# An RWKV/gMLP trunk: projections as 512-column products per channel tile, and six row copies a batch moved from ScalarE to DMA

## The chip, the cores and the metric

One core of one Trainium2 chip runs the kernel. The metric is the device time of one execution in microseconds (us). TensorE (PE) multiplies, VectorE (DVE) and ScalarE (ACT) do the elementwise work, GpSimd (POOL) a little of it, SyncE (SP) issues most DMAs. Products land in PSUM, whose banks hold 512 float32 numbers in each of 128 partitions; everything else lies in SBUF.

## The reference

The input is 256 tokens of width 2048 in float32. Two residual layers follow each other, then a last RMS norm.

```python
def rwkv7_bidir_mixer(h, w_in, mu_prev, mu_next, ...):      # layer 0
    z = h @ w_in                       # 2048 -> r, k, v (4096 each), 4 low-rank inputs of 96, gate (4096)
    zs, gate = z[..., :SHIFT_COLS], z[..., SHIFT_COLS:]
    zs = zs + mu_prev * (shift_prev(zs) - zs) + mu_next * (shift_next(zs) - zs)
    ...
    for d, rev in ((0, False), (1, True)):                  # one scan per direction, 64 heads of 64
        # S_t = S_{t-1} diag(w_t) + (S_{t-1} a_t) b_t^T + v_t k_t^T ;  y_t = S_t r_t
        y = y + wkv_scan(rh, heads(decay), kd_h, vh, -kk, kk * a_h, rev)
        bonus = bonus + jnp.sum(rh * kd_h * r_k, axis=-1, keepdims=True) * vh
    ...                                                     # group norm of y, plus bonus
    return (out * jax.nn.silu(gate)) @ w_out                # 4096 -> 2048

def chunked_sgu_mixer(h, w_in, ln_g, ln_b, w_s, b_s, w_out):  # layer 1
    u, v, gate = jnp.split(h @ w_in, 3, axis=-1)            # 2048 -> 3 x 4096
    ...                                                     # spatial mix of v in chunks of 128 tokens
    return (u * s * jax.nn.silu(gate)) @ w_out
```

## The kernel before

**Precision by three products.** Every float32 operand of a large product is split into a hi and a lo part of type float32r. `mm3` (L163) adds up hi·hi, lo·hi and hi·lo in one PSUM bank. The activations of layer 0 are split into `zT`, two tiles `zh` and `zl` of 16 k-tiles by 256 tokens.

**Weights.** `want` queues up a piece of a weight matrix, `prefetch` keeps three pieces ready, `fetch` hands out the next. `convert` (L133) makes one: a DMA on SP's queue into one of two raw buffers (L145; L143 for the low-rank ones), a cast on ScalarE to the hi part (L150), a subtraction on VectorE for the lo part (L151). A raw buffer is free for the next DMA when L151 has read it. A piece holds 1024 numbers per partition, 512 KB. `want_cols` (L173) cuts a column range of a weight matrix into such pieces; for a width of 256 it is four k-tiles of 256 columns, in runs of 1 KB.

**Rounds.** The 4096 channels are worked on in 16 batches of 256 (two channel tiles of 128, four heads). Round p of the loop at L909 interleaves generators, each of which yields its due time within a round of nominally 78: the projections (`mains`) of k and r of batch p and of v and gate of batch p-1; `rates`, `factors` and `early_grams` of batch p; `before` (grams of the second direction, then `inverses`), `values` and `transposed_factors` of batch p-1; `after` (the scan over four chunks of 64 tokens, `chain`, then `finish`) of batch p-2. The due times set the order in which instructions are written; a scheduler then orders each engine's queue by its own model of the times. Each engine, and SP's DMA queue, works through its queue in order.

**A projection.** `mains` takes one PSUM bank for a segment of a batch: 256 tokens of the first channel tile, then 256 of the second. `project` (L179) runs the 16 k-tiles, and for each the two channel tiles, three products of 256 columns each:

```python
mm3(acc, (hi[:, j, cs], lo[:, j, cs]), (zT[0][:, k], zT[1][:, k]), k == 0 and i % 2 == 0, k == KT - 1)
```

Two banks of the tag "acc" alternate. Then `shifted` (L390 to L399) makes the token shift for r, k and v straight from PSUM: for each channel tile one ScalarE activation and two VectorE steps. The gate takes one activation (L450) and one VectorE step (L451) over both tiles.

**The wide product.** In layer 1, u and gate use `project_wide` (L194). There the activations lie as hi and lo side by side, so that hi weights meet 512 columns at once (L204) and lo weights only the 256 hi columns (L206). Its two halves are then summed by a ScalarE copy (L1065) and a VectorE add (L1066).

**The inverses.** `inverses` (L611) copies 32-row blocks of the gram matrix `Gs` to `Dt` (L623) and `NQ` (L624), solves for triangular inverses on VectorE (L627 to L643), finishes off the off-diagonal block by products into `qp` (L651, L657), and puts together `TTs` from `qp` (L660) and from the transposed `TD` (L661, L662). All these copies move 32 partitions by 512 numbers and run on ScalarE. `TTs` is one buffer, read by `chain` at L722 (`uu`). `values` (L684) then has SP's queue overwrite half of `Gs` from `AR`, which must wait for the copies out of `Gs`, and fill `RC`.

Of the kernel before, what the change touches and what calls it, by code (L numbers as in the profile page):

```python
# [22 lines left out]
def trunk(tc, x, norm_g, final_norm_g, w_in, mu_prev, mu_next, w0, w_up, a0, a_up, k_k, k_a, r_k,  # L23
# [149 lines left out]
    def want_cols(w, c_off, b, name):  # L173
        a = min(KT, 1 << int(math.log2(RAW // b)))
        wv = w.rearrange("(k p) c -> p k c", p=P)
        for k0 in range(0, KT, a):
            want(wv[:, k0:k0 + a, c_off:c_off + b], a, b, f"{name}{k0}")
# [32 lines left out]

    def acc_pair(name):
        return sm(name, "acc").rearrange("p (i t) -> p i t", i=2)
# [69 lines left out]
    zT = (zp.tile([P, KT, T], F32R, tag="zh", name="zh"), zp.tile([P, KT, T], F32R, tag="zl", name="zl"))  # L282
# [73 lines left out]
    for todo in plan:  # L356
        for s, b in todo:
            if s == "u":
                want([w_[0, :, :, b * 2 * P:(b + 1) * 2 * P].rearrange("d k c -> k d c") for w_ in (w_up, a_up)],
                     4, 2 * P, f"wu{b}")  # L360
            else:
                want_cols(w_in, segment[s] + b * 2 * P, 2 * P, f"w{s}{b}_")
# [27 lines left out]
    def shifted(acc, dst, b, m):  # L390

        for cl in range(2):
            a = acc[:, cl]
            j = m * NCT + 2 * b + cl
            S.activation(dst[:, cl], a, AF.Identity, scale=c0[:, j:j + 1])
            V.scalar_tensor_tensor(dst[:, cl, 1:], a[:, :T - 1], col["mp"][:, j:j + 1], dst[:, cl, 1:],
                                   ALU.mult, ALU.add)
            V.scalar_tensor_tensor(dst[:, cl, :T - 1], a[:, 1:], col["mn"][:, j:j + 1], dst[:, cl, :T - 1],
                                   ALU.mult, ALU.add)  # L399
# [36 lines left out]
    def mains(todo, st):  # L436
        slot = dict(k=0, r=4, g=12, v=8) if "k" in dict(todo) else dict(v=0, g=4)
        last = -4
        for s, b in todo:
            if s == "u":  # L440
                st[b]["wu"] = fetch()
                continue
            last = max(last + 4, slot[s])
            yield last * MT
            acc = acc_pair(f"acc{s}{b}")
            for i, _ in enumerate(project(2 * P, [acc[:, 0], acc[:, 1]], zT)):
                yield last * MT + i * dt
            if s == "g":
                SG = fr.tile([P, 2, T], F32, tag="SG", name=f"SG{b}", bufs=2)
                S.activation(SG, acc, AF.Tanh, scale=0.5)  # L450
                V.scalar_tensor_tensor(SG, SG, 1.0, acc, ALU.add, ALU.mult)  # L451
                st[b]["SG"] = SG
            elif s == "v":
                Vt = fr.tile([P, 2, T], F32, tag="Vt", name=f"Vt{b}", bufs=2)
                shifted(acc, Vt, b, 2)
                st[b]["Vt"] = Vt
            else:
                t = fr.tile([P, 2, T], F32, tag=f"{s}t", name=f"{s}t{b}")
                shifted(acc, t, b, dict(r=0, k=1)[s])
                st[b][dict(r="Rt", k="Kt")[s]] = t  # L460
# [150 lines left out]
    def inverses(b, f):  # L611
# [8 lines left out]
        for h in range(2):  # L620
# [3 lines left out]
            S.copy(NQ[h * 64:h * 64 + 32], Gs[0:32, h, :, 32:64])  # L624
# [30 lines left out]
        for u in range(16):  # L655
            for h in range(2):
                PE.matmul(qp[R0[h], u], NQ[R1[h], u], TD[R1[h], u], start=True, stop=True)  # L657
        yield TQ[1] + 2
        for h in range(2):
            S.copy(TTs[R0[h], h, :, 32:64], qp[R0[h]])  # L660
            S.copy(TTs[R0[h], h, :, 0:32], TD[R0[h]])  # L661
            S.copy(TTs[R1[h], h, :, 32:64], TD[R1[h]])  # L662
# [206 lines left out]
    def early_out():  # L869

        yield 4
        oA = [zp.tile([P, HE, T], F32R, tag=t, name=f"{t}_o0") for t in ("zh", "zl")]
# [196 lines left out]
    pA = [zp.tile([P, HE, T], F32R, tag=t, name=f"{t}_o1") for t in ("zh", "zl")]  # L1069
# [101 lines left out]
```

## Time and profile before

| | |
|---|---|
| median of 3 runs | 2230.92 us (2229.87 to 2234.58) |
| the profiled execution | 2229.16 us |
| its span, first to last instruction | 2227.4 us |
| mean granted TensorE clock | 0.995 |
| TensorE / VectorE / ScalarE busy | 98% / 72% / 60% of the span |
| layer 0 with its projections | about 31 to 1290 us of the span |
| output of layer 0, then layer 1 | 1290 us to the end |

How to read the lines of a profile: L12 is line 12 of the kernel; `out<-in` names what is written and what is read. A line of a group gives the shapes, the count behind x, busy time in us, the mean duration of one in ns, then the idle time of that engine just before, and what ended it. A line of a stretch gives the busy time of each engine in it, with the number of instructions, the granted clock, the busy share of the DMA engines and GB/s. A line of a wait gives total us, number of times and the longest. A line of the timeline gives start and duration in us. A line of a DMA issue gives count, size, and median us to landing. TensorE's products overlap, so the duration of one isn't its price.

### The profile page before, as it was taken

The page shows a single profiled execution, that of the slowest core. Times are in us where ns is not written, and L with a number is a line of the kernel's source. Part 1 is how long each engine was busy: PE and PEld are TensorE (multiplying, and loading weights), DVE is VectorE, ACT ScalarE, POOL GpSimd, SP SyncE. Part 2 cuts the span into 40 slices and gives each one's busy share as a digit, 9 for nine tenths or more (in the row PEclk, how much of TensorE's full clock was granted, in tenths as well). Part 3 has the DMA queues.
Part 4 walks back from the last instruction along what each step waited for, and adds up shares of the span by engine and source line. Part 5 has one row for each costly group of instructions (what it writes and reads, how often), then busy time and mean ns, then how long its engine had stood idle before and what let it go on. Part 6 is the DMA issues. An engine that isn't in the chain of part 4 may idle for free.

```text
span 2227.4 us, 48630 instructions
## 1 busy us (share of the span) xinstructions
PE 2179.0 (98%) x19984; PEld 1944.7 (87%) x19984; DVE 1608.1 (72%) x3121; ACT 1345.2 (60%) x2128; POOL 171.8 (8%) x230
## 2 busy tenths in 40 slices
PE   7999999999999999999999999999999999999998
PEld 7889999999999999999999877778888888888886
DVE  5797788787977977887888764465546777777444
ACT  6556777777767676776767664464444444444443
POOL 2210110011001101100010000000000000000000
PEclk9999999999999999999999999999999999999999
DMA  5555444454445544444545555586766666665664
GB/s 167 140 145 142 109 126 134 125 137 112 130 127 143 139 126 131 129 125 136 137 124 138 167 174 177 173 263 189 221 204 190 198 189 195 195 193 192 195 198 154
DMA packets 352687, 356.01 MB, mean 160 GB/s; under 512 B 78160, under 2 KB 300112, under 8 KB 352336
## 3 DMA queue, kind: packets, MB, share of 16 engines
q1 hardware_dynamic: 332208, 331.66, 51.6%
q10 hardware_dynamic: 20256, 21.24, 3.2%
q8 instruction: 157, 2.57, 0.5%
q14 instruction: 66, 0.54, 0.1%
HBM read 329.78 MB, written 6.29 MB: 151 GB/s over the span
## 4 chain that ended last, share of the span: by engine, by line
PE 69%; ACT 10%; DMA 9%; DVE 8%; issue 3%; ACTq 0%; SPq 0%; POOL 0%; POOLq 0%; DVEq 0%
PE uacc L204 5%; PE gacc L204 5%; DMA raw_o<-in_rwkv_w_out_dram 3%; PE oacc L166 3%; PE oacc L167 3%; PE oacc L165 3%; PE gp L584 3%; PE gacc L206 3%; PE uacc L206 3%; PE vacc L167 3%; PE vacc L165 3%; PE vacc L166 3%; ACT Dt L623 2%; PE accv L165 2%; PE accg L167 2%
## 5 line engine op out<-in xcount | busy, mean ns | idle before, releaser
L204 PE MATMUL uacc<-z,whi_u 128*128 128x512 f32 x512 | 179.0, 394 | 0.0
L204 PE MATMUL gacc<-z,whi_g 128*128 128x512 f32 x512 | 177.3, 393 | 0.0
L167 PE MATMUL accg<-zh,wlo_wg 128*128 128x256 f32 x512 | 149.6, 292 | 2.5 <-DVE wlo_wg L151 2.4
L165 PE MATMUL accv<-zh,whi_wv 128*128 128x256 f32 x512 | 149.2, 291 | 1.1 <-ACT whi_wv L150 1.1
L167 PE MATMUL accr<-zh,wlo_wr 128*128 128x256 f32 x512 | 148.7, 290 | 0.6 <-DVE wlo_wr L151 0.5
L165 PE MATMUL acck<-zh,whi_wk 128*128 128x256 f32 x512 | 148.1, 289 | 1.1 <-ACT whi_wk L150 1.1
L165 PE MATMUL accr<-zh,whi_wr 128*128 128x256 f32 x512 | 149.0, 291 | 0.0
L165 PE MATMUL accg<-zh,whi_wg 128*128 128x256 f32 x512 | 148.4, 290 | 0.0
L166 PE MATMUL accr<-zl,whi_wr 128*128 128x256 f32 x512 | 148.1, 289 | 0.0
L167 PE MATMUL accv<-zh,wlo_wv 128*128 128x256 f32 x512 | 147.5, 288 | 0.1
L167 PE MATMUL acck<-zh,wlo_wk 128*128 128x256 f32 x512 | 146.2, 286 | 1.0 <-DVE wlo_wk L151 1.0
L166 PE MATMUL accv<-zl,whi_wv 128*128 128x256 f32 x512 | 147.2, 287 | 0.0
L166 PE MATMUL accg<-zl,whi_wg 128*128 128x256 f32 x512 | 147.0, 287 | 0.0
L166 PE MATMUL acck<-zl,whi_wk 128*128 128x256 f32 x512 | 147.0, 287 | 0.0
L206 PE MATMUL uacc<-z,wlo_u 128*128 128x256 f32 x512 | 142.4, 284 | 0.0
L206 PE MATMUL gacc<-z,wlo_g 128*128 128x256 f32 x512 | 140.2, 279 | 0.0
L151 DVE TENSOR_TENSOR wlo_v<-raw_v,whi_v 128x1024 fp32r<-128x1024 f32 x64 | 78.4, 1225 | 80.4 <-ACT whi_v L150 80.4
L151 DVE TENSOR_TENSOR wlo_o<-raw_o,whi_o 128x1024 fp32r<-128x1024 f32 x64 | 78.2, 1224 | 77.5 <-ACT whi_o L150 77.2
L639 DVE TENSOR_TENSOR X<-X,TD 128x126 f32<-128x126 f32 (+22 forms) x496 | 126.5, 255 | 9.4
L637 DVE TENSOR_TENSOR TD<-La,X 128x126 f32<-128x126 f32 (+22 forms) x496 | 125.6, 253 | 10.6
L151 DVE TENSOR_TENSOR wlo_p<-raw_p,whi_p 128x1024 fp32r<-128x1024 f32 x60 | 73.9, 1232 | 75.7 <-ACT whi_p L150 75.7
L150 ACT CAST whi_p<-raw_p 128x1024 fp32r<-128x1024 f32 x60 | 63.1, 1051 | 91.5 <-PE oacc L167 87.3
(331 smaller groups left out, 6842.3 us busy)
## 6 DMA issues: line engine op xcount, KB each, us to landing
raw_wk<-in_rwkv_w_in_dram SPq DMA_DIRECT2D x64, 512.0 KB, 3.7
raw_wr<-in_rwkv_w_in_dram SPq DMA_DIRECT2D x64, 512.0 KB, 3.7
raw_wv<-in_rwkv_w_in_dram SPq DMA_DIRECT2D x64, 512.0 KB, 3.7
raw_wg<-in_rwkv_w_in_dram SPq DMA_DIRECT2D x64, 512.0 KB, 3.7
raw_o<-in_rwkv_w_out_dram SPq DMA_DIRECT2D x64, 512.0 KB, 4.0
raw_v<-in_gmlp_w_in_dram SPq DMA_DIRECT2D x64, 512.0 KB, 3.7
raw_u<-in_gmlp_w_in_dram SPq DMA_DIRECT2D x64, 512.0 KB, 3.5
raw_g<-in_gmlp_w_in_dram SPq DMA_DIRECT2D x64, 512.0 KB, 3.6
```

What stands on the lines that cost most here:

```text
L150: latest[0] = S.copy(hi, raw)
L151: latest[1] = V.tensor_tensor(lo, raw, hi.bitcast(F32), ALU.subtract)
L165: PE.matmul(acc, a[0], b[0], start=first, stop=False, skip_group_check=True)
L166: PE.matmul(acc, a[0], b[1], start=False, stop=False, skip_group_check=True)
L167: PE.matmul(acc, a[1], b[0], start=False, stop=last, skip_group_check=True)
L204: PE.matmul(acc.rearrange("p h t -> p (h t)"), hi[:, j, cs], zc[:, k].rearrange("p h t -> p (h t)"), start=k == 0, stop=False, skip_group_ ...
L206: PE.matmul(acc[:, 0], lo[:, j, cs], zc[:, k, 0], start=False, stop=k == KT - 1, skip_group_check=True)
L584: PE.matmul(gp[h][:, c].rearrange("p q t -> p (q t)"), BK[H[h], d, cl, c].rearrange("p q t -> p (q t)"), AR[H[h], d, cl, c].rearrange("p q ...
L623: S.copy(Dt[r0:r0 + 32].rearrange("p t u -> p u t"), Gs[q * 32:q * 32 + 32, h, :, q * 32:q * 32 + 32])
L637: V.tensor_tensor(tv, La[:, j, 0:j].unsqueeze(2).to_broadcast([P, j, n]), X[:, j:j + 1, m:].to_broadcast([P, j, n]), ALU.mult)
L639: V.tensor_tensor(X[:, 0:j, m:], X[:, 0:j, m:], tv, ALU.add)
```

## The change

**Projections.** The weights of r, k, v and gate are wanted 128 columns at a time, eight k-tiles a piece, in runs of 512 bytes. `zT` becomes two views of one tile `zi` in which hi and lo lie side by side. Each channel tile takes a PSUM bank of its own and `project_wide`; a ScalarE copy and a VectorE add sum the halves into `pa` in SBUF, one buffer, from which the shift or the gate's steps work for that channel tile.

**Copies.** In `inverses`, the two copies to `NQ` and the four copies from `TD` to `TTs` become DMAs issued on SP's queue. The copies from `Gs` to `Dt` and from `qp` stay.

Later tiles that took over the space of `zh` and `zl` now take the two halves of one tile; nothing else changes there.

```diff
     def want_cols(w, c_off, b, name):
-        a = min(KT, 1 << int(math.log2(RAW // b)))
+        a = min(KT, RAW // b if b == P else 1 << int(math.log2(RAW // b)))
...
-    zT = (zp.tile([P, KT, T], F32R, tag="zh", name="zh"), zp.tile([P, KT, T], F32R, tag="zl", name="zl"))
+    zi = zp.tile([P, KT, 2, T], F32R, tag="z", name="z0")
+    zT = [zi[:, :, i] for i in range(2)]
...
-                want_cols(w_in, segment[s] + b * 2 * P, 2 * P, f"w{s}{b}_")
+                for cl in range(2):
+                    want_cols(w_in, segment[s] + (2 * b + cl) * P, P, f"w{s}{b}_{cl}")
...
-    def shifted(acc, dst, b, m):
-
-        for cl in range(2):
-            a = acc[:, cl]
-            j = m * NCT + 2 * b + cl
-            S.activation(dst[:, cl], a, AF.Identity, scale=c0[:, j:j + 1])
-            V.scalar_tensor_tensor(dst[:, cl, 1:], a[:, :T - 1], col["mp"][:, j:j + 1], dst[:, cl, 1:],
-                                   ALU.mult, ALU.add)
-            V.scalar_tensor_tensor(dst[:, cl, :T - 1], a[:, 1:], col["mn"][:, j:j + 1], dst[:, cl, :T - 1],
-                                   ALU.mult, ALU.add)
+    def shifted(a, dst, j):
+
+        S.activation(dst, a, AF.Identity, scale=c0[:, j:j + 1])
+        V.scalar_tensor_tensor(dst[:, 1:], a[:, :T - 1], col["mp"][:, j:j + 1], dst[:, 1:], ALU.mult, ALU.add)
+        V.scalar_tensor_tensor(dst[:, :T - 1], a[:, 1:], col["mn"][:, j:j + 1], dst[:, :T - 1], ALU.mult, ALU.add)
...
-            acc = acc_pair(f"acc{s}{b}")
-            for i, _ in enumerate(project(2 * P, [acc[:, 0], acc[:, 1]], zT)):
-                yield last * MT + i * dt
-            if s == "g":
-                SG = fr.tile([P, 2, T], F32, tag="SG", name=f"SG{b}", bufs=2)
-                S.activation(SG, acc, AF.Tanh, scale=0.5)
-                V.scalar_tensor_tensor(SG, SG, 1.0, acc, ALU.add, ALU.mult)
-                st[b]["SG"] = SG
...
+            tag, n = dict(k=("kt", 1), r=("rt", 1), v=("Vt", 2), g=("SG", 2))[s]
+            dst = fr.tile([P, 2, T], F32, tag=tag, name=f"{tag}{b}", bufs=n)
+            for cl in range(2):
+                acc = sm(f"acc{s}{b}_{cl}", "acc").rearrange("p (h t) -> p h t", h=2)
+                for i, _ in enumerate(project_wide(P, [acc], zi)):
+                    yield last * MT + (cl * KT + i) * dt / 2
+
+                a = fr.tile([P, T], F32, tag="pa", name=f"pa{s}{b}_{cl}")
+                S.copy(a, acc[:, 1])
+                V.tensor_tensor(a, acc[:, 0], a, ALU.add)
+                if s == "g":
+                    S.activation(dst[:, cl], a, AF.Tanh, scale=0.5)
+                    V.scalar_tensor_tensor(dst[:, cl], dst[:, cl], 1.0, a, ALU.add, ALU.mult)
+                else:
+                    shifted(a, dst[:, cl], dict(r=0, k=1, v=2)[s] * NCT + 2 * b + cl)
+            st[b][dict(r="Rt", k="Kt", v="Vt", g="SG")[s]] = dst
...
-            S.copy(NQ[h * 64:h * 64 + 32], Gs[0:32, h, :, 32:64])
+            nc.sync.dma_start(NQ[h * 64:h * 64 + 32], Gs[0:32, h, :, 32:64])
...
                 PE.matmul(qp[R0[h], u], NQ[R1[h], u], TD[R1[h], u], start=True, stop=True)
+        for h in range(2):
+            nc.sync.dma_start(TTs[R0[h], h, :, 0:32], TD[R0[h]])
+            nc.sync.dma_start(TTs[R1[h], h, :, 32:64], TD[R1[h]])
         yield TQ[1] + 2
         for h in range(2):
             S.copy(TTs[R0[h], h, :, 32:64], qp[R0[h]])
-            S.copy(TTs[R0[h], h, :, 0:32], TD[R0[h]])
-            S.copy(TTs[R1[h], h, :, 32:64], TD[R1[h]])
```

More of the change, by code (lines that the diff above doesn't have):

```diff
@@ L209, in project_wide @@
                 yield
-    def acc_pair(name):
-        return sm(name, "acc").rearrange("p (i t) -> p i t", i=2)
     n3 = 3 * NCT
@@ L444, in mains @@
             yield last * MT
-            acc = acc_pair(f"acc{s}{b}")
-            for i, _ in enumerate(project(2 * P, [acc[:, 0], acc[:, 1]], zT)):
-                yield last * MT + i * dt
-            if s == "g":
-                SG = fr.tile([P, 2, T], F32, tag="SG", name=f"SG{b}", bufs=2)
-                S.activation(SG, acc, AF.Tanh, scale=0.5)
-                V.scalar_tensor_tensor(SG, SG, 1.0, acc, ALU.add, ALU.mult)
-                st[b]["SG"] = SG
[L453 to L460, printed above, removed]
+            tag, n = dict(k=("kt", 1), r=("rt", 1), v=("Vt", 2), g=("SG", 2))[s]
[13 more added lines that the diff above has]
+            st[b][dict(r="Rt", k="Kt", v="Vt", g="SG")[s]] = dst
         if ("g", NB - 1) in todo:
@@ L871, in early_out @@
         yield 4
-        oA = [zp.tile([P, HE, T], F32R, tag=t, name=f"{t}_o0") for t in ("zh", "zl")]
+        oA = zp.tile([P, 2, HE, T], F32R, tag="z", name="z_o0")
+        oA = [oA[:, i] for i in range(2)]
         oC = sc.tile([P, 2, 16, 2 * C], F32R, tag="Gs", name="oCh", bufs=2)
@@ L1067, in gated @@
         V.tensor_tensor(dst, dst, rb2, ALU.mult)
-    pA = [zp.tile([P, HE, T], F32R, tag=t, name=f"{t}_o1") for t in ("zh", "zl")]
+    pA = zp.tile([P, 2, HE, T], F32R, tag="z", name="z_o1")
+    pA = [pA[:, i] for i in range(2)]
     pB = None
```

## The prediction

> **What bounds the kernel now.** I read the page first (busy shares, the chain that ended last), then the sums by stage, TensorE's waits in the steady part of the RWKV layer, and its timeline there and in the gMLP layer, which already has the wide product.
>
> ```profile
> span 2227.4 us, 48630 instructions
> PE 2179.0 (98%) x19984; PEld 1944.7 (87%) x19984; DVE 1608.1 (72%) x3121; ACT 1345.2 (60%) x2128; POOL 171.8 (8%) x230
> PE 69%; ACT 10%; DMA 9%; DVE 8%; issue 3%; ACTq 0%; SPq 0%; POOL 0%; POOLq 0%; DVEq 0%
> ```
>
> TensorE carries 69% of the chain. A busy TensorE alone says little, since products overlap; so the stages:
>
> ```profile
> core 0: us, PE busy (x) PEld busy (x) DVE busy (x) ACT busy (x) POOL busy (x), PEclk, DMA share, GB/s
> 58.00:290.00 232.00, 219.88 (x2330) 208.03 (x2330) 190.29 (x389) 151.57 (x248) 34.28 (x37) 0.97 0.49 134
> 600.00:1221.00 621.00, 615.91 (x7639) 574.47 (x7638) 508.87 (x1195) 442.15 (x765) 58.23 (x79) 1.00 0.50 132
> ...
> PE yp L731 <- ACT SUV L724: 2.1, 2, 1.1
> PE uu L722 <- ACT Xs L718: 1.9, 4, 0.6
> PE xp L713 <- ACT SUV L680: 0.6, 2, 0.3
> ```
>
> 600 to 1221 us holds eight rounds of one batch each, 77.6 us a round. TensorE idles 5.1 us in eight rounds, 4.6 of them in three waits on ScalarE, none on a weight. VectorE is busy 63.6 us a round (82%), ScalarE 55.3. So here a round is as long as TensorE's work in it. From 58 to 290 (rounds 1 to 3) TensorE idles 12.1 us and its clock was 0.97: there other engines still matter.
>
> **The projections.** One unit (one k-tile, one channel tile) is now three 256-column products; it becomes one of 512 and one of 256. Both exist in the trace, uninterrupted:
>
> ```profile
> 642.39 0.28 PE L165 MATMUL accr<-zh,whi_wr 128*128 128x256 f32 x1
> 642.51 0.28 PE L166 MATMUL accr<-zl,whi_wr 128*128 128x256 f32 x1
> 642.63 0.28 PE L167 MATMUL accr<-zh,wlo_wr 128*128 128x256 f32 x1
> ...
> 644.19 0.28 PE L165 MATMUL accr<-zh,whi_wr 128*128 128x256 f32 x1
> ```
>
> ```profile
> 1753.33 0.39 PE L204 MATMUL gacc<-z,whi_g 128*128 128x512 f32 x1
> 1753.56 0.28 PE L206 MATMUL gacc<-z,wlo_g 128*128 128x256 f32 x1
> ...
> 1755.07 0.39 PE L204 MATMUL gacc<-z,whi_g 128*128 128x512 f32 x1
> ```
>
> From 642.39 to 644.19 stand five old units: 360 ns each, 120 a product. From 1753.33 to 1755.07 stand five new ones: 348 ns each (231 and 117). The saving is 12 to 13 ns a unit; I take 12.5. Durations (0.28, 0.39) are not the price, the distance between starts is.
>
> ```profile
> L165 PE MATMUL acck<-zh,whi_wk 128*128 128x256 f32 x512 | 148.1, 289 | 1.1 <-ACT whi_wk L150 1.1
> L1065 ACT COPY Gt<-uacc 128x256 f32<-128x256 f32 x32 | 12.0, 374 | 16.8 <-PE uacc L206 16.8
> L1066 DVE TENSOR_TENSOR U<-uacc,Gt 128x256 f32<-128x256 f32 x32 | 13.5, 421 | 2.1 <-ACT Gt L1065 0.7
> L661 ACT COPY TTs<-TD 32x512 f32<-32x512 f32 x32 | 19.7, 615 | 17.4 <-DVE TD L642 8.0 <-PE uu L722 7.8 <-DVE nm L760 1.4
> L624 ACT COPY NQ<-Gs 32x512 f32<-32x512 f32 x32 | 19.8, 618 | 3.6 <-DVE Gs L589 3.0
> L450 ACT ACTIVATE SG<-accg 128x512 f32<-128x512 f32 x16 | 9.7, 607 | 0.1
> L451 DVE SCALAR_TENSOR_TENSOR SG<-SG,accg 128x512 f32<-128x512 f32 x16 | 10.9, 682 | 9.0 <-ACT SG L450 9.0
> L395 ACT ACTIVATE kt<-acck,c 128x256 f32<-128x256 f32 x32 | 15.3, 477 | 5.2 <-PE acck L167 3.6 <-DVE kt L398 1.3
> L492 ACT ACTIVATE SQ<-kt,pc 128x256 f32<-128x256 f32 x32 | 16.2, 506 | 2.4 <-DVE kt L398 2.4
> L568 DVE SCALAR_TENSOR_TENSOR BQ<-rt,pc,TH 128x256 f32<-128x256 f32 x32 | 14.1, 469 | 0.0
> ```
>
> 512 products of each kind and segment, four segments: 2048 units, 128 a round. 2048 x 12.5 ns = **25.6 us off TensorE**, 1.6 a round. At 98 to 99% busy that is on the path.
>
> **What it adds.** The two halves of a bank must be summed: per channel tile one ScalarE copy from PSUM (nearest row L1065, 0.374 us) and one VectorE add (L1066, 0.421); eight channel tiles a round.
> - VectorE: 8 x 0.421 = 3.4 us; the gate's 512-wide step (0.682) becomes two of 256 (L568, 0.469 each): +0.26. The shift steps stay. Together +3.6: 67.2 us a round, against 76.0 us left to TensorE, 88%.
> - ScalarE: +8 x 0.374 = 3.0; the gate's activation 0.607 becomes 2 x 0.506 (L492): +0.4; six of the shift's activations read SBUF (0.506) instead of PSUM (0.477): +0.2. Off go six copies of 0.617 (two as L624, four as L661): -3.7. Net about zero.
> - The bank: a unit row of 16 k-tiles lasts 16 x 0.348 = 5.6 us alone and 9.5 us with the other work of the round, and two banks alternate. Copy and add hold a bank 0.8 us plus two queue waits (L450 shows 9.0 us over 16 behind it). Zero. The one `pa` buffer makes the next copy wait for the shift of the last tile: copy, add, activation, two steps, 2.2 us without waits, under 9.5. If queue waits push that over 9.5 plus a bank's 5.6, TensorE stops; I leave that in the VectorE rival.
>
> What hides VectorE's 3.6 us is its idle time, 14.0 us a round (621 less 508.87, by eight), which falls to 8.8. Bounds of the cost: 0 (all hidden) to 16 x 3.6 = 58 us (none). TensorE idles 0.64 us a round today, none of it named for VectorE; if that grows as VectorE's idle shrinks, 0.64 x 14.0/8.8 = 1.0, it is +0.4 a round. Rounds 1 to 3 have less cover. I take **+6 us** in all.
>
> **Weight loads.** Each load keeps 512 KB but runs of 512 bytes (128 columns), twice as many.
>
> ```profile
> raw_wk<-in_rwkv_w_in_dram SPq DMA_DIRECT2D x64, 512.0 KB, 3.7
> RC<-AR SPq DMA_DIRECT2D x32, 256.0 KB, 5.2
> Gs<-AR SPq DMA_DIRECT2D x32, 256.0 KB, 3.7
> L684 SPq DMA_DIRECT2D Gs<-AR x32: 590/596/665, 108.5 to 1256.3; - x32
> ```
>
> The nearest rows are those two, 1024 runs of 256 bytes in 3.7 to 5.2 us, against 512 runs of 1 KB in 3.7. So a load lands 0 to 1.5 us later; I take 0.3, near the lower end, since half of the DMA time is free (share 0.50). In steady rounds it is hidden (no TensorE wait on a weight above); where two raw buffers pace the start, about a dozen loads, it is exposed: bounds 0 to 18 us, taken **+2**.
>
> **The six row copies.** The four TTs copies and two NQ copies become DMAs on SP, each 64 KB in runs of 128 bytes. Issue: 6 x 0.6 us (L684) a round, against seventeen weight issues; room enough. Landing: bounds 3.7 to 5.2 us by the rows above, against 0.617.
>
> ```profile
> 924.36 0.62 ACT L661 COPY TTs<-TD 32x512 f32<-32x512 f32 x1 [2.04 <-DVE TD L642]
> ...
> 952.50 0.69 PE L722 MATMUL uu<-Xs,TTs 128*64 128x64 f32 x16
> ...
> SPq L684 <- ACT NQ L624: 46.4, 20, 5.7
> SPq L684 <- DVE Gs L589: 19.6, 9, 5.8
> ```
>
> TTs could start at 924 and is read at 952: 28 us cover 5.2. NQ is read half a round later; but Gs<-AR overwrites what NQ copies, so SP now holds that DMA until ScalarE has done NQ (46.4 us in 20 waits). Afterwards it waits for four Dt copies and a landing instead; ScalarE ends 1.2 us earlier, the landing may take it back: zero, bounds -1 to +2 a round, off TensorE's path. What is new is order: SP waits in line for TD and the last uu before it issues the weight loads behind. Cost now: zero; see the SP rival.
> [...]
>
> **Sum**, against the profiled execution (2229.16 us, span 2227.4): 2229.2 - 25.6 + 6 + 2 = 2211.6. The median of the runs is 1.8 above it: **2213 us**, 0.8% faster.
>
> **Rivals.**
> - Full gain: VectorE's idle takes everything, and ScalarE without the bursts of four and two copies shortens its waits (4.6 us in eight rounds, 9 in sixteen). 2231 - 25.6 - 9 = 2196. For it: no VectorE name among TensorE's waits. Against: VectorE at 88%.
> - Columns set the price, not products: if the 512 takes 2 x 120 here and the 256 after it 120, as all rows of this stage do, a unit stays at 360, nothing is saved and the 8 us of costs stay: 2239. Against it: 231 and 117 on the same engine at the same clock; the one difference is the interruptions by small products.
>   [...]
> - VectorE sets the round (slower). A round is then 67.2 us plus the waits VectorE can't shed. It decides when these exceed 76.0 - 67.2 = 8.8 us (10.4 and it is slower than 77.6). The steady waits that the rows below name make 6.2 us; all of today's idle is 14.0. At 11.5: 78.7, +1.1 a round, 2231 + 18 + 2 = 2251.
>
> ```profile
> DVE La L627 <- ACT Dt L623: 28.8, 8, 4.5
> DVE wlo_wk L151 <- ACT whi_wk L150: 20.4, 16, 4.3
> ```
>
> - SP's line (slower). Three converted tiles last 3 x 24 x 0.12 = 8.6 us at full projection speed; a load needs 3.7 and two conversions. A wait over about 3 us a round, in front of a load, is exposed; the longest such wait now is 5.8. At 2.5 us a round: 2213 + 40 = 2253.
>
> **How the numbers follow.** Forecast (2201 to 2225) 0.57; full gain 0.13; columns 0.13; VectorE 0.11; SP 0.06. No change means within 0.2%, 4.5 us, about what a measurement of this kernel can tell. The columns case spreads from 2226 to 2239 as its 8 us of costs are paid or hidden: 0.02 faster, 0.06 no change, 0.05 slower; the forecast's upper costs give 0.03 to no change. Faster: 0.54 + 0.13 + 0.02 = 0.69. Same: 0.09. Slower: 0.11 + 0.06 + 0.05 = 0.22. The range leaves out the far ends of both slower cases and of the full gain: 2192 to 2242; the forecast's own is 2201 to 2225.
>
> **What would show it.** Right: project_wide rows with 2048 products of 512 and 256 columns, starts 231 and 117 ns apart; a steady round of 76 us; VectorE near 67 a round; TensorE idle about 1 us a round; no wait on TTs. Wrong: 512-column products 240 apart; VectorE at 90% and above with TensorE waiting for `pa` or wlo; half-clock stretches; or SP's new issues waiting for TD with raw loads behind them.

## The result, and the profile after

| | before | after |
|---|---|---|
| median, same chip | 2232.52 us | 2268.97 us (2268.44 to 2273.37) |
| ratio | | 1.0168, 95% interval [1.0150, 1.0186] |
| profiled span | 2227.4 us | 2266.7 us |
| mean granted TensorE clock in it | 0.995 | 0.987 |
| first product of layer 0's output (`oacc`) | 1275.1 us | 1300.8 us |
| first product of layer 1's v (`vacc`) | 1495.3 us | 1534.4 us |

The change makes the kernel 1.7% slower; forecast were 2213 us, in a range of 2192 to 2242. Of the 39 us between the two profiled executions, 25.7 arise before the first product of layer 0's output and 13.4 in the stage behind it, which still holds the scan of the last batches; the rest of layer 1 takes 732 us in both.

The 39 us can be added up another way. TensorE stands idle for 83.1 us of the span instead of 48.4: 8.6 us of the increase lie before 600 us, 15.8 from 600 to 1221 us, 10.3 behind that. Stretches at half clock take some 18 us more in this execution, and the wide products save some 12 (both worked out below). That makes about 41, as near as the clock is known.

Nor does the loss grow evenly from round to round. ScalarE's copy that opens the scan of a batch (`yp<-smask`) starts 6.1 us later than before in the second batch (252.0, 258.1), 44.7 later in the eighth (690.5, 735.2) and 43.8 later in the fifteenth (1242.5, 1286.4). The first k product of the last batch is only 6.2 us late (1163.1, 1169.3). So in the new order of instructions the scan trails further behind the projections.

The page of the kernel after, the lines that answer to those of before:

```profile
span 2266.7 us, 45076 instructions
PE 2183.6 (96%) x17936; PEld 1834.4 (81%) x17936; DVE 1648.2 (73%) x3265; ACT 1325.2 (58%) x2176; POOL 193.1 (9%) x230
PE 60%; DVE 15%; DMA 11%; ACT 9%; issue 3%; POOL 0%; SPq 0%; ACTq 0%; POOLq 0%; DVEq 0%
```

The products went from 19984 to 17936, as meant. But TensorE's part of the chain fell from 69 to 60%, and VectorE's rose from 8 to 15%. The stretches of the kernel after:

```profile
core 0: us, PE busy (x) PEld busy (x) DVE busy (x) ACT busy (x) POOL busy (x), PEclk, DMA share, GB/s
58.00:290.00 232.00, 215.76 (x1870) 184.85 (x1869) 192.40 (x397) 148.46 (x253) 40.89 (x37) 0.95 0.52 135
600.00:1221.00 621.00, 600.10 (x6474) 501.15 (x6473) 518.52 (x1248) 424.43 (x776) 70.36 (x80) 1.00 0.53 134
```

In the same 621 us TensorE now idles 20.9 us instead of 5.1. A steady round, from the first k product to that of the next round, takes 78.9 us (mean of the six from 695.8 us); before, the six from 699.2 us took 77.3 on average. VectorE is busy 84% of the stretch, 66.1 us a round. What TensorE waits for there, the five largest of 20.5 us in all:

```profile
PE qp L645 <- DVE Tn L637: 6.1, 8, 1.2
PE accv L206 <- DVE wlo_wv L151: 5.9, 8, 0.8
PE vp L668 <- ACT TTs L657: 3.5, 8, 0.4
PE accv L204 <- ACT whi_wv L150: 1.8, 2, 1.3
PE uu L717 <- ACT Xs L713: 1.7, 5, 0.7
```

Two of the five are weights, which TensorE did not wait for in this stretch before. The timeline of TensorE in the kernel after, the first and the last of five units in a row:

```profile
640.26 0.40 PE L204 MATMUL accr<-z,whi_wr 128*128 128x512 f32 x1
640.49 0.28 PE L206 MATMUL accr<-z,wlo_wr 128*128 128x256 f32 x1
640.61 0.40 PE L204 MATMUL accr<-z,whi_wr 128*128 128x512 f32 x1
...
642.03 0.40 PE L204 MATMUL accr<-z,whi_wr 128*128 128x512 f32 x1
```

Five units take 1.77 us, 354 ns each, not 348. The groups of the added operations (last column: idle time of the engine just before, and what ended it):

```profile
L447 ACT COPY pak<-acck 128x256 f32<-128x256 f32 x32 | 11.8, 369 | 43.1 <-DVE mv L750 31.1 <-DVE kt L393 10.1 <-PE acck L206 1.8
L448 DVE TENSOR_TENSOR par<-accr,par 128x256 f32<-128x256 f32 x32 | 13.4, 419 | 27.5 <-ACT par L447 27.5
```

Both cost in themselves what was forecast (0.369 and 0.419 us). But in front of k's copies ScalarE stands idle for 43.1 us, 41 of them until VectorE has got through its queue, and in front of r's adds VectorE stands 27.5 us until ScalarE has copied.

### The profile page after: what moved, and what is told of

It is laid out like the page before. It is cut to its first block, busy times and chain, and to the rows that moved or that the text cites. A ratio compares the mean times of both kernels' runs of the same rounds, so it can differ in the third digit from the quotient of the medians.

```text
span 2266.7 us, 45076 instructions
## 1 busy us (share of the span) xinstructions
PE 2183.6 (96%) x17936; PEld 1834.4 (81%) x17936; DVE 1648.2 (73%) x3265; ACT 1325.2 (58%) x2176; POOL 193.1 (9%) x230
## 4 chain that ended last, share of the span: by engine, by line
PE 60%; DVE 15%; DMA 11%; ACT 9%; issue 3%; POOL 0%; SPq 0%; ACTq 0%; POOLq 0%; DVEq 0%
PE uacc L204 5%; PE gacc L204 5%; PE oacc L166 4%; PE oacc L167 4%; PE acck L204 4%; PE oacc L165 4%; PE gacc L206 3%; PE uacc L206 3%; PE vacc L167 3%; PE vacc L165 3%; PE vacc L166 3%; PE accg L204 3%; DMA raw_wv<-in_rwkv_w_in_dram 2%; DMA raw_wk<-in_rwkv_w_in_dram 2%; PE accv L204 2%
## 5 line engine op out<-in xcount | busy, mean ns | idle before, releaser
L204 PE MATMUL accr<-z,whi_wr 128*128 128x512 f32 x512 | 194.7, 415 | 0.0
L204 PE MATMUL accv<-z,whi_wv 128*128 128x512 f32 x512 | 185.5, 399 | 2.7 <-ACT whi_wv L150 2.6
L204 PE MATMUL acck<-z,whi_wk 128*128 128x512 f32 x512 | 185.8, 402 | 2.3 <-ACT whi_wk L150 2.3
L204 PE MATMUL accg<-z,whi_wg 128*128 128x512 f32 x512 | 186.3, 402 | 0.0
L206 PE MATMUL accv<-z,wlo_wv 128*128 128x256 f32 x512 | 147.4, 288 | 7.3 <-DVE wlo_wv L151 7.3
L206 PE MATMUL accg<-z,wlo_wg 128*128 128x256 f32 x512 | 147.4, 288 | 5.3 <-DVE wlo_wg L151 5.3
L206 PE MATMUL acck<-z,wlo_wk 128*128 128x256 f32 x512 | 148.6, 290 | 1.8 <-DVE wlo_wk L151 1.8
L206 PE MATMUL accr<-z,wlo_wr 128*128 128x256 f32 x512 | 149.1, 291 | 0.2 <-DVE wlo_wr L151 0.2
L151 DVE TENSOR_TENSOR wlo_o<-raw_o,whi_o 128x1024 fp32r<-128x1024 f32 x64 | 78.2, 1224 | 78.9 <-ACT whi_o L150 78.8
L151 DVE TENSOR_TENSOR wlo_p<-raw_p,whi_p 128x1024 fp32r<-128x1024 f32 x60 | 73.9, 1232 | 75.7 <-ACT whi_p L150 75.7
L578 PE MATMUL gp<-AR,BK 64*128 64x128 f32 x1024 | 111.3, 295 | 9.1 <-DVE Gs L583 9.1
L204 PEld LDWEIGHTS accr<-z,whi_wr 128*128 128x128 f32 x512 | 99.0, 193 | 22.1 <-issue 0.2
L204 PEld LDWEIGHTS acck<-z,whi_wk 128*128 128x128 f32 x512 | 96.8, 189 | 24.6 <-ACT whi_wk L150 2.7
```

The lines of the kernel that those rows point to most:

```text
L151: latest[1] = V.tensor_tensor(lo, raw, hi.bitcast(F32), ALU.subtract)
L204: PE.matmul(acc.rearrange("p h t -> p (h t)"), hi[:, j, cs], zc[:, k].rearrange("p h t -> p (h t)"), start=k == 0, stop=False, skip_group_ ...
L206: PE.matmul(acc[:, 0], lo[:, j, cs], zc[:, k, 0], start=False, stop=k == KT - 1, skip_group_check=True)
L578: PE.matmul(gp[h][:, c].rearrange("p q t -> p (q t)"), BK[H[h], d, cl, c].rearrange("p q t -> p (q t)"), AR[H[h], d, cl, c].rearrange("p q ...
```

## The experiments

Eighteen kernels, each timed against before on the same chip. The last two columns split the time: every run has its span and its mean granted clock, and span x (1 - clock) is what the stretches at half clock (0.50 in every one shown below) take if all their time is spent on products ("clock"), span x clock is the remainder ("rest"). Both are medians over the runs; the clock is known to 0.001, which is 2.2 us.

| kernel | us | ratio, 95% interval | clock | rest |
|---|---|---|---|---|
| before (50 runs) | 2230.6 | 1 | 11.1 | 2218.3 |
| after | 2268.97 | 1.0168 [1.0150, 1.0186] | 36.3 | 2232.2 |
| copies_only | 2210.31 | 0.9909 [0.9885, 0.9932] | 11.0 | 2198.4 |
| proj_only | 2288.28 | 1.0258 [1.0232, 1.0283] | 59.5 | 2226.0 |
| nq_act | 2269.28 | 1.0178 [1.0151, 1.0205] | 44.2 | 2225.3 |
| proj_256 | 2350.05 | 1.0528 [1.0499, 1.0558] | 62.2 | 2285.7 |
| three_nosum | 2219.10 | 0.9948 [0.9933, 0.9963] | 17.7 | 2200.7 |
| wide_nosum | 2236.90 | 1.0023 [1.0011, 1.0035] | 22.4 | 2212.6 |
| three_sum | 2243.72 | 1.0067 [1.0046, 1.0089] | 24.7 | 2219.9 |
| pa_two | 2257.39 | 1.0124 [1.0107, 1.0141] | 47.4 | 2207.3 |
| three_nosum_fix | 2216.92 | 0.9937 [0.9921, 0.9953] | 11.1 | 2204.4 |
| wide_nosum_fix | 2220.79 | 0.9955 [0.9934, 0.9976] | 15.5 | 2202.6 |
| three_sum_fix | 2265.26 | 1.0152 [1.0129, 1.0175] | 35.1 | 2228.3 |
| wide_sum_fix | 2252.68 | 1.0097 [1.0079, 1.0115] | 12.4 | 2238.4 |
| copy_only_fix | 2255.14 | 1.0117 [1.0099, 1.0134] | 29.3 | 2225.2 |
| load_only_fix | 2248.98 | 1.0087 [1.0072, 1.0102] | 21.3 | 2225.9 |
| wide_sum_pool_fix | 2274.52 | 1.0199 [1.0182, 1.0216] | 40.9 | 2230.8 |
| copies_pool | 2276.28 | 1.0208 [1.0189, 1.0226] | 63.7 | 2211.7 |
| act_only_fix | 2249.77 | 1.0072 [1.0036, 1.0109] | 38.2 | 2206.6 |
| dve_only_fix | 2227.95 | 0.9981 [0.9969, 0.9992] | 8.9 | 2215.5 |

### The two halves of the change, and SP's line

My first theory was the order on SP's queue: the DMA of `NQ` stands between others there, with weight loads behind. The row of SP's waits in the kernel after that carried it:

```profile
SPq L679 <- DMA NQ<-Gs: 76.1, 30, 4.7
```

The rival was VectorE, loaded by the adds. Four kernels: the copies alone, the projections alone, the change with `NQ` back on ScalarE, and the projections with pieces of 256 columns.

copies_only: before, with

```diff
-            S.copy(NQ[h * 64:h * 64 + 32], Gs[0:32, h, :, 32:64])
+            nc.sync.dma_start(NQ[h * 64:h * 64 + 32], Gs[0:32, h, :, 32:64])
...
+            nc.sync.dma_start(TTs[R0[h], h, :, 0:32], TD[R0[h]])
+            nc.sync.dma_start(TTs[R1[h], h, :, 32:64], TD[R1[h]])
-            S.copy(TTs[R0[h], h, :, 0:32], TD[R0[h]])
-            S.copy(TTs[R1[h], h, :, 32:64], TD[R1[h]])
```

> The kernel before with only the six row copies as DMAs on SP; projections as before. Theory SP (the two NQ DMAs and the two Gs<-AR DMAs wait for each other in SP's line, so that a weight load behind them is issued late): slower by 1.1 to 2 us a round, 2248 to 2262 us, with Gs<-AR waiting for NQ's landing on SP and a load of wv or wr landing late. Theory VectorE (the extra 3.6 us a round of adds make it late): 2228 to 2236 us, nothing changes. Theory order (the planner finds another order, and that is what costs): anything, without those waits.

Measured 2210.31 us: a gain of 20, which only the theory of order left room for, in rounds of 75.7 us. In the same stretch as above TensorE has next to nothing left to wait for (stretch, then TensorE's waits in it):

```profile
600.00:1221.00 621.00, 620.57 (x7875) 580.81 (x7874) 527.09 (x1225) 428.37 (x740) 55.35 (x85) 1.00 0.54 140
```

```profile
PE yp L732 <- ACT SUV L725: 0.4, 1, 0.4
```

The same six DMAs on the same queue speed the kernel up, so SP's line is not what costs. TensorE's idle time fell by only 0.6 of the 1.6 us that a round lost. Its scan products `yp` and `xp` also stand closer together (those groups are busy 47.7 us in six rounds, before 57.6), so part of the waiting stood inside TensorE's busy time. The scheduler made another order here too; how much that gave was not tested. This is also the fastest kernel of all that were run.

nq_act: after, with only this line taken back

```diff
-            nc.sync.dma_start(NQ[h * 64:h * 64 + 32], Gs[0:32, h, :, 32:64])
+            S.copy(NQ[h * 64:h * 64 + 32], Gs[0:32, h, :, 32:64])
```

> The changed kernel with only the two NQ copies back on ScalarE, TTs still by DMA. Theory SP puts the cost on NQ alone: 2216 to 2236 us, as with all six back. If the four TTs DMAs cost too (SP waiting for TD): above that by 10 us or more. Theory VectorE: 2255 to 2270 us.

2269.28 us: no change. The theory fell here a second time: SP's 76.1 us are spent, but nobody waits for them.

proj_only: after, with all six copies on ScalarE (the diff of copies_only backwards).

> The changed kernel with all six row copies back on ScalarE; projections wide, a channel tile at a time. Theory SP: the wait for the wv load is gone and what is left is the saving of 6 ns a unit (354 against 360 ns) seen in the changed kernel's trace, 2048 x 6 = 12 us: 2216 to 2232 us. Theory VectorE: stays slow, 2250 to 2270 us, VectorE's work per round being the same as in the changed kernel.

2288.28 us, 58 more than before and above the ranges of both theories. -20 and +58 give the +38 of the change: its halves add up, and the projections carry all the loss.

proj_256: proj_only, with weights again in runs of 1 KB, two channel tiles side by side, each with its bank

```diff
-                for cl in range(2):
-                    want_cols(w_in, segment[s] + (2 * b + cl) * P, P, f"w{s}{b}_{cl}")
+                want_cols(w_in, segment[s] + b * 2 * P, 2 * P, f"w{s}{b}_")
...
-                for i, _ in enumerate(project_wide(P, [acc], zi)):
+            for i, _ in enumerate(project_wide(2 * P, accs, zi)):
```

> Wide projections with all six copies on ScalarE, but weights in pieces of 256 columns (runs of 1 KB) and both channel tiles going together on two banks, as in the gMLP layer. If the price of the 512-column product (236 ns instead of 231) hangs on the pieces of 128 columns, it is 231 here and the time is 6 to 12 us under the kernel with the 128-column pieces. Against that, both banks are then held at the end of a segment, so TensorE waits for the copy and add at each of four segments a round: if that decides, 1 us a segment, 64 us more.

2350.05 us, 62 more than proj_only: far worse, about as expected. It takes both banks at once, so that the next segment waits for copy and add (13.1 us of TensorE's waits from 600 to 1150 us end on the adds into `pa`). Five units in a row (645.78 to 647.56 us) take 356 ns each, so the dearer 512-column product doesn't hang on pieces of 128 columns. A channel tile at a time is the better form; the runs of 512 bytes can't be judged by it.

### The product and the sum apart

With the six copies by DMA in all of them: the product in three pieces of 256 columns or wide, and with or without copy and add. Without them the shift reads PSUM as before. wide_nosum leaves out the lo half of the activations; three_sum adds the lo products into the other half of the bank, so that the sum is needed.

```diff
-                for i, _ in enumerate(project_wide(P, [acc], zi)):
+                for i, _ in enumerate(project(P, [acc[:, 0]], zT)):
...
-                a = fr.tile([P, T], F32, tag="pa", name=f"pa{s}{b}_{cl}")
-                S.copy(a, acc[:, 1])
-                V.tensor_tensor(a, acc[:, 0], a, ALU.add)
+                a = acc[:, 0]
```

(both edits: three_nosum; the second alone: wide_nosum; the first alone, with the lo products into `acc[:, 1]`: three_sum)

> Copies by DMA; three 256-column products as before into half a bank, but a channel tile at a time with weights in pieces of 128 columns, and the shift straight from PSUM. Only the order of the work and the 512-byte runs differ from the copies alone. Theory sum and theory buffer: 2205 to 2220 us. Theory tile (half as long a time to empty a bank, shorter runs): 2250 us or more.

> The changed kernel without the ScalarE copy and VectorE add: the shift and the gate read the first half of the bank from PSUM, so the product of hi weights with lo activations is computed and left out of the result. Theory sum (the copy and add, and what waits for them, cost the 58 us that the projections' half costs alone): 2195 to 2215 us, below the copies alone (2210) by up to the 12 us of the wide product. Theory form (512-column products or a channel tile at a time cost it): 2250 us or more. Theory buffer (the one pa buffer): like theory sum, since pa is gone.

> As the changed kernel, but with three 256-column products, hi and lo into the two halves of a bank, then the same copy and add. Theory sum and theory buffer: 2270 to 2290 us (the changed kernel plus the 12 us of the wide product). Theory form: 2205 to 2220 us.

From copies_only, a channel tile at a time costs 8.8 us (2219.1). From there the wide product costs 17.8 (2236.9), where 25.6 of gain were forecast, and the sum 24.6 (2243.7); on top of the wide product the sum costs 32.1 (2269.0). wide_nosum and three_sum lie in no theory's range. The surprise was the wide product's price, and the order of the instructions was a suspect, as the scheduler sets it by its own model of the times.

pa_two: after, with two `pa` buffers.

```diff
-                a = fr.tile([P, T], F32, tag="pa", name=f"pa{s}{b}_{cl}")
+                a = fr.tile([P, T], F32, tag="pa", name=f"pa{s}{b}_{cl}", bufs=2)
```

> The changed kernel with two pa buffers instead of one. Theory buffer (ScalarE's copy to pa stands in its queue until VectorE has shifted the last tile out of it: 20.7 us of ScalarE's waits in six rounds of the changed kernel): 2215 to 2240 us, and that wait gone. Theory sum: 2260 to 2275 us, unchanged.

2257.39 us as the median of three executions (2256.29 to 2261.01), 12 less than after and between the two theories; a fourth took 3256.87 us at a mean clock of 0.591, for which nothing here gives a reason, and is left out. The stretch from 600 to 1221 us:

```profile
600.00:1221.00 621.00, 611.11 (x6519) 516.61 (x6519) 525.69 (x1252) 428.98 (x775) 62.25 (x78) 0.98 0.52 134
```

TensorE idles 9.9 us instead of 20.9, but its clock fell from 1.00 to 0.98. In the table: the rest falls by 25 us, the clock takes 11 more. So the one buffer was a true cause of waits, but about half of what the second gave was taken back, and a round still takes 78.8 us.

### The same four with the order held fixed

The scheduler's model of the times was switched off in four more kernels; the order of TensorE's work then agrees to 99.5% among them.

```diff
-    with _tile.TileContext(nc, schedule_with_timeline_sim=True) as tc:
+    with _tile.TileContext(nc, schedule_with_timeline_sim=False) as tc:
```

> Three 256-column products, no copy and add, a channel tile at a time, copies by DMA; each engine's order now follows from the due times alone, not from the scheduler's timing model. The base of four kernels whose TensorE order is the same to 99.5%, counted in units of products. No theory sets its time; it may be well above 2219 us.

> The same with the wide products (again the lo activations' half is left out of the result). Theory order (the wide products lost 18 us because the scheduler's model gave another order, with too little work ahead of the scan's products): here the order is the same, so the wide form is faster, by up to 6 ns a unit, 12 us, if TensorE sets the pace, and not slower than by 3 us. Theory form (512-column products are dearer in themselves, or block TensorE for what waits behind them): slower by 10 to 25 us here too.

> The base with copy and add. Theory sum (the chain copy, add, activation, two steps through one pa buffer costs time in itself): slower than the base by 20 us or more. Theory order: within 8 us of the base.

> The changed kernel in the same fixed order. Theory form and theory sum together: 38 us or more above the base. Theory order: within 10 us of the base. Sum alone: about as the base with copy and add, less up to 12 us.

Without the sum, three products or the wide one take the same: 2216.92 and 2220.79 us (the latter from 2213.79 to 2226.64), rounds of 75.0 and 75.1. So the loss of 18 goes with the scheduler's order, not with the wide product as such. But there is no gain either. TensorE's one wait between 600 and 1150 us, first with three products, then wide:

```profile
PE qp L649 <- ACT NQ L645: 6.4, 8, 0.9
```

```profile
PE qp L649 <- ACT NQ L645: 13.0, 8, 1.6
```

Eight times 0.8 us more: just what the wide product saves in a round (128 units of 6 ns). (`NQ` is here the half of that tile which ScalarE still copies, from `qp`, between the two products that finish the inverses; the half moved to DMA is the other.) TensorE gets there earlier and waits for ScalarE's `NQ`. The round is set by what stands ahead of that copy, not by TensorE, though TensorE is busy 99 and 98% of the time.

With the sum: 2265.26 and 2252.68, that is +48 and +32. In three_sum_fix the same wait is 2.7 us long, in each round:

```profile
PE qp L663 <- ACT NQ L659: 19.1, 7, 2.7
```

and after it the clock drops (stretches of that kernel around one such wait, columns as above; the one after POOL is the granted clock):

```profile
619.00:623.50 4.50, 1.76 (x60) 1.55 (x60) 4.50 (x9) 4.16 (x7) 0.88 (x3) 1.00 0.54 140
623.50:626.90 3.40, 3.40 (x64) 3.22 (x60) 2.94 (x4) 2.73 (x6) 0.00 (x0) 0.50 0.42 122
626.90:630.00 3.10, 3.10 (x31) 2.98 (x30) 2.97 (x5) 1.52 (x3) 0.00 (x0) 1.00 0.63 183
```

3.4 us at half clock, in every round (the mean clock from 600 to 1150 us is 0.98): 1.7 us lost. With the 1.8 us by which the wait grew (2.7 against 0.9) that is the 3.5 us that a round grew (75.0 to 78.5).

### Which of copy and add

Theories for the sum's price: VectorE's load; the path from PSUM over `pa`; and later ScalarE's copy. Of wide_sum_fix, copy_only_fix leaves out the add (and the lo half), load_only_fix lets the shift read PSUM while copy and add go into a tile that nothing reads (the lo half doesn't count there either). Two kernels give part of VectorE's steps to GpSimd.

```diff
-                S.copy(a, acc[:, 1])
-                V.tensor_tensor(a, acc[:, 0], a, ALU.add)
+                S.copy(a, acc[:, 0])
```

> The changed kernel in the fixed order, with ScalarE copying the first half of the bank to pa and no VectorE add (the lo activations' half is left out of the result). Theory VectorE's load: a round of 75 us as without copy and add, 2213 to 2226 us. Theory path (the pa buffer and one more engine change in the way of the shift) or ScalarE's copy: 77 us a round, 2245 to 2258 us.

```diff
+                a = acc[:, 0]
...
+                x = fr.tile([P, T], F32, tag="pa", name=f"pa{s}{b}_{cl}")
+                S.copy(x, acc[:, 1])
+                V.tensor_tensor(x, acc[:, 0], x, ALU.add)
```

> The changed kernel in the fixed order, with the shift and the gate straight from PSUM, and behind them the copy and the add into pa, which nobody reads (the lo half is left out of the result). Theory VectorE's load: 77 to 78.5 us a round, 2243 to 2268 us, as with the sum in the path. Theory path: 75 us a round, 2213 to 2228 us.

2255.14 without the add, so no gain in time: by the split the rest falls by 13.2 us and the clock takes 16.9 more. 2248.98 with nobody reading the sum: that the shift waits for the sum is only the smaller part (3.7 us of the 31.9). But load_only_fix doesn't part load from path wholly. The bank is held until the unread add has read it, and that is what TensorE waits for there:

```profile
PE acck L204 <- DVE pag L454: 14.4, 7, 2.1
```

These 2.1 us a round stand in place of the 1.6 for `NQ`, which are gone. In wide_sum_fix the same wait is 0.5 us a round, beside others on ScalarE's `SUV` (1.0) and VectorE's weights (0.6).

```diff
-    EB, DK, LAST = 2, 4, 8
+    EB, DK, LAST = 16, 4, 8
```

> The changed kernel in the fixed order, with five 512-wide products a round (the lines that use eng, 0.68 us each on VectorE) on GpSimd in all batches instead of the first two. Theory VectorE's load: 3.4 us a round less for VectorE, so the round falls from 77.2 to 74 to 75.5 us, 2205 to 2230 us, unless GpSimd's slower steps come into the way. Theory path: unchanged, 2245 us or more.

> The kernel before with the six copies by DMA and those five VectorE steps a round on GpSimd, scheduled with the timing model as before. If VectorE sets the 75.7 us of its round: 73 to 75 us a round, 2170 to 2200 us. If TensorE does (busy throughout): 2205 to 2215 us. Slower if GpSimd's steps are late.

2274.52 (22 more than wide_sum_fix) and 2276.28 (66 more than copies_only). Such a step takes 1.5 to 2.0 us on GpSimd in the first two batches of before, against 0.68 on VectorE in the others, so GpSimd's are probably in the way, which wasn't taken apart; in wide_sum_pool_fix the rest did fall by 7.6 us, and the clock took 28.5. Stretch from 600 to 1150 us of that kernel, then of wide_sum_fix:

```profile
600.00:1150.00 550.00, 526.99 (x5762) 448.12 (x5759) 461.62 (x1073) 381.75 (x688) 107.09 (x105) 0.97 0.52 135
```

```profile
600.00:1150.00 550.00, 532.68 (x5896) 447.83 (x5895) 474.06 (x1143) 387.14 (x704) 52.15 (x72) 1.00 0.53 137
```

Last, each engine's addition by itself, unread, in wide_nosum_fix:

```diff
+                x = fr.tile([P, T], F32, tag="pa", name=f"pa{s}{b}_{cl}")
+                S.copy(x, acc[:, 1])            # act_only_fix
+                V.tensor_copy(x, acc[:, 1])     # dve_only_fix, in its place
```

> The 512-column form with the order of issue fixed, shift and gate reading PSUM, and per channel tile one ScalarE copy of the bank's lo half into a tile that nothing reads (the sum is left out, so the lo activations do not reach the output). The same kernel without that copy took 2220.8 us with rounds of 75.1 us; with that copy and a VectorE add, also unread, it took 2249.0 with rounds of 77.3. Theory A (it is ScalarE's added copy, 8 x 0.37 us a round in ScalarE's in-order queue, ahead of the weight conversions and of the scan's steps): 2243 to 2256, rounds of 76.8 to 78. Theory B (it is VectorE's added operation, 8 x 0.42 us): 2215 to 2228, rounds of 75.1. If neither alone does it and both together do, both this run and the next stand at 2215 to 2230.

> As the kernel before it in this group, but with one VectorE copy of the bank's lo half per channel tile into a tile that nothing reads, and no ScalarE copy (the sum is left out here too). Theory A (ScalarE's added copy): 2215 to 2228, rounds of 75.1 us. Theory B (VectorE's added operation): 2243 to 2256, rounds of 76.8 to 78. If each engine's addition costs a part, both kernels lie between, near 2235.

ScalarE's copy alone: 2249.77, +29. VectorE's operation alone: 2227.95, +7. So ScalarE's eight copies of 0.37 us a round are enough for a loss as large as that of both together. It is a loss of another kind, though. Against wide_nosum_fix, ScalarE's copy adds 4 us to the rest and 23 to the clock; VectorE's operation adds 13 to the rest and nothing to the clock; both together (load_only_fix) add 23 to the rest and 6 to the clock. So the engines' shares in the sum's price can't be read from these two times alone.

How ScalarE's copy costs, the profiled execution shows. ScalarE's timeline up to `NQ`, in act_only_fix and then in wide_nosum_fix:

```profile
613.49 0.37 ACT L453 COPY pav<-accv 128x256 f32<-128x256 f32 x1
613.76 1.06 ACT L150 CAST whi_wg<-raw_wg 128x1024 fp32r<-128x1024 f32 x1
614.72 1.09 ACT L535 ACTIVATE TH<-TA,kab,pc 128x256 f32<-128x256 f32 x2
615.83 1.17 ACT L647 COPY NQ<-qp 32x512 f32<-32x512 f32 x2
```

```profile
672.40 1.09 ACT L150 CAST whi_wg<-raw_wg 128x1024 fp32r<-128x1024 f32 x1
673.34 1.13 ACT L533 ACTIVATE TH<-TA,kab,pc 128x256 f32<-128x256 f32 x2
674.50 1.17 ACT L645 COPY NQ<-qp 32x512 f32<-32x512 f32 x2
```

The added copy stands in the queue just ahead of the work that leads to `NQ`. TensorE's timeline at the wait for `NQ`, in act_only_fix and then in wide_nosum_fix (in brackets the idle time before, and its end):

```profile
614.56 0.28 PE L206 MATMUL accg<-z,wlo_wg 128*128 128x256 f32 x1
614.77 0.33 PE L771 MATMUL yt<-ident,yn 128*64 128x64 f32 x2
617.04 1.17 PE L651 MATMUL qp<-TD,NQ 32*32 32x32 f32 x36 [1.95 <-ACT NQ L647]
```

```profile
673.79 0.28 PE L206 MATMUL accg<-z,wlo_wg 128*128 128x256 f32 x1
675.72 1.20 PE L649 MATMUL qp<-TD,NQ 32*32 32x32 f32 x64 [1.64 <-ACT NQ L645]
```

And the stretches around them, again in that order:

```profile
609.00:616.90 7.90, 6.10 (x62) 5.03 (x55) 6.73 (x11) 6.43 (x16) 2.72 (x5) 1.00 0.43 107
616.90:623.70 6.80, 6.66 (x113) 6.16 (x114) 5.13 (x9) 3.80 (x7) 3.82 (x1) 0.50 0.55 155
```

```profile
668.00:675.70 7.70, 6.07 (x75) 5.08 (x68) 6.36 (x11) 6.35 (x16) 2.52 (x5) 1.00 0.47 116
675.70:682.50 6.80, 6.78 (x131) 6.13 (x132) 6.80 (x11) 5.14 (x8) 4.80 (x1) 1.00 0.56 159
```

The wait is 0.3 us longer, and TensorE then runs 6.8 us at half clock: 3.4 us, in each of the rounds (the mean clock from 600 to 1150 us is 0.96), which last 78.5 us instead of 75.1. In the profiled executions this is nearly the whole price: about 45 us more lost to the clock (58.7 against 13.3, each known to 2.2), 44.6 us more span. The five executions of this one kernel bear it out: 2239.18 us at a clock of 0.987, 2241.37 at 0.985, 2249.77 at 0.983, 2250.99 at 0.981, 2259.81 at 0.974. Over the 50 runs of before (clock 0.992 to 0.997) the time goes up 0.86 us for each us of the column "clock".

VectorE's operation, by contrast, took nothing by the clock and lengthened the round to 76.2 us: its price is all in the rest.

The half-clock stretches shown here last 3.4 us (three_sum_fix), 6.8 us (act_only_fix), and 10.2 and 13.7 us (after). A single wait of 2.7 us (three_sum_fix) and one of 1.95 us (act_only_fix) were each followed by such a stretch, one of 1.64 us (wide_nosum_fix) by none.

## Why the prediction was wrong, point by point

**The two steps that failed.** The sum of the two halves was priced at 6 us, all of it VectorE's, with ScalarE, the bank and `pa` at nothing. It costs 25 to 48 us in four pairs of kernels. And a saving of 25.6 us on TensorE was put on the path; half of it exists, and with the order fixed none of it reaches the time. From copies_only over three_nosum and wide_nosum to after, the terms measure: copies -20.3 (forecast 0), a channel tile at a time with shorter runs +8.8 (+2), wide product +17.8 (-25.6), sum +32.1 (+6). They add up to the +38 of the change against the median of all runs of before.

**The saving on TensorE, 25.6 us.** Mis-sized, and then not on the path. A unit takes 354 ns, not 348: 12.3 us over 2048 units. The layer 1 rows that I took (231 and 117 ns) didn't carry over; here the 512-column product takes 236 and the other 118. Why 5 ns more is open. And with the order fixed, what it saves turns into waiting for `NQ`. What failed is "at 98 to 99% busy that is on the path". In the fixed order the work ahead of `NQ` was just as long as TensorE's, so shortening the one alone gained nothing.

**"ScalarE net zero".** The balance of busy time was about right: 1345.2 to 1325.2 us, 1.2 us a round less. But equal busy time isn't equal price. Taking the six copies away gained 20 us, in the scheduler's own order; putting the eight in by themselves cost 29, in the fixed one, most of it by the clock. A copy of 0.37 us delays what stands behind it in ScalarE's queue, as the timelines ahead of `NQ` show. The waits of TensorE before, in the steady rounds, which I had quoted, all ended on ScalarE (4.6 us in eight rounds). They were a sign of that, however small.

**The six copies at zero.** They gained 20.3 us; only the full-gain rival had the direction, with 9. Landing took 3.5 to 3.7 us, the lower end of the forecast:

```profile
TTs<-TD SPq DMA_DIRECT2D x64, 64.0 KB, 3.7
NQ<-Gs SPq DMA_DIRECT2D x32, 64.0 KB, 3.5
```

**VectorE, +6 us.** An operation like its add costs 7.2 us by itself, so this size was near. VectorE's busy time rose by 2.5 us a round, not 3.6. But with ScalarE's copy the price is 28 to 32 on the wide product in the fixed order, and ScalarE's copy is what my sum left at nothing.

**The one `pa` buffer, zero unless queue waits push it.** They did: pa_two took 25 us off the rest, of which 12 were left in the time.

**Weight loads, +2.** By its own working the term should have been 3.6 (0.3 us on a dozen loads). A channel tile at a time costs 8.8 us in all (three_nosum against copies_only), of which the runs of 512 bytes are some part, and 6.7 of which are clock by the split; the load itself went from 3.7 to 3.9 us:

```profile
raw_wk<-in_rwkv_w_in_dram SPq DMA_DIRECT2D x64, 512.0 KB, 3.9
```

**The rivals.** "VectorE sets the round" gave the right sign and, with 78.7 us, nearly the round of 78.9. VectorE is busy 66.1 us of it (67.2 by the rival), and 12.0 of the 20.5 us that TensorE waits from 600 to 1221 us end on VectorE. That its load alone does it isn't borne out by the fixed order: the operation by itself costs 7 us, and leaving out the add gains no time. In the changed kernel's own order this wasn't tested. "SP's line" fell. "Columns set the price" holds by half (354 stands between 348 and 360).

**What I hadn't priced: the clock.** Half-clock stretches stand among the signs of a wrong forecast, without a term. Of the change's 39 us by the split, 25 are clock (11.1 to 36.3) and 14 the rest; in the profiled execution, at a clock of 0.987, it is about 18 and 21. Where they are in the kernel after (two of ten stretches before the last 10 us, and the wait ahead of the second):

```profile
94.60:108.30 13.70, 11.53 (x48) 10.49 (x49) 9.45 (x16) 5.88 (x9) 1.68 (x3) 0.50 0.39 98
1282.40:1292.60 10.20, 9.82 (x61) 8.41 (x63) 5.23 (x10) 6.34 (x15) 0.33 (x1) 0.50 0.29 86
```

```profile
1279.40 0.66 PE L668 MATMUL vp<-ident,Vt 128*128 128x128 f32 x4 [1.30 <-ACT TTs L657]
1282.78 0.58 PE L578 MATMUL gp<-AR,BK 64*128 64x128 f32 x1 [2.72 <-DVE Gs L583]
```

None lies in the steady rounds from 600 to 1221 us, where the loss (78.9 against 77.3) is waits alone; six lie in the first rounds, up to 480 us, and four around the change to the output stage, which gives part of the 13.4 us lost there (the stage in before, then in after):

```profile
1275.10:1495.30 220.20, 213.84 (x1465) 167.47 (x1466) 121.21 (x189) 115.38 (x179) 4.96 (x5) 0.99 0.62 197
```

```profile
1300.80:1534.40 233.60, 221.57 (x1547) 173.23 (x1546) 129.17 (x218) 115.11 (x181) 4.35 (x5) 0.98 0.59 187
```

TensorE is busy 7.7 us longer there and idles 5.7 us longer.

**What stays open.** The clock was not set in any run, so its share is an arithmetic split, supported by the spread within one kernel, not a test. In copy_only_fix and load_only_fix the rest is 23 us above wide_nosum_fix, where ScalarE's copy alone adds 4 and VectorE's operation alone 13; how they combine was not taken apart. So which engine carries how much of the sum's price is open, and in the changed kernel's own order most of all. The wide product's 18 us in the scheduler's own order are put down to order since they vanish in the fixed one; which shift of order does it was not tried. The traces show one: the last row of g products starts at 1214.0 us in three_nosum and at 1216.8 in wide_nosum, but the scan of the fifteenth batch (`yp<-smask`) at 1223.8 and 1257.5.

## What to carry to other kernels

An engine that is busy 98% of the time need not be the limit: if its few waits all end on the same other engine, that engine's queue may set the round. Try to relieve that first (here six small copies moved to DMA gave 0.9%), and count an addition to an engine's queue by what stands behind it (here eight copies of 0.37 us a round: 29 us), not by the balance of busy time. And where TensorE runs with short waits only, price a wait that gets longer at its length plus a possible stretch at half clock (in act_only_fix 0.3 us more of wait, and 3.4 us lost behind it).

## What the runs showed of the hardware

- A wait of TensorE of 1.64 us was followed by no drop in the clock (wide_nosum_fix), one of 1.95 us by 6.8 us at half clock (act_only_fix) and one of 2.7 us by 3.4 us (three_sum_fix), in each kernel round after round; so here the length of the stretch doesn't follow from the length of the wait.
- The same instructions in the same order took from 2239.18 to 2259.81 us (act_only_fix), in step with the granted clock.
- A 512-column product took 231 ns from start to start in layer 1 (before) and 236 in layer 0 (after), on one engine at a clock of 1.00.
- Six DMAs of 64 KB a round in runs of 128 bytes, from SBUF to SBUF, cost nothing that showed beside the gain of 20.3 us (copies_only).
